# Moving small steps of a hybrid encoder block: latent scaling, first weights, rope table and buffer turns

## The chip, the cores and the metric

The kernel runs on one core of a Trainium2 chip. The core has five engines with queues of their own: TensorE (PE in the profile) multiplies matrices, VectorE (DVE) and ScalarE (ACT) work element by element, GpSimd (POOL) does small side work, and SyncE (SP) issues nearly all DMA transfers. Each engine executes its instructions in order; between engines there are only semaphores. The metric is the device time of one execution in microseconds (us), and the median of several executions is compared.

## The reference, cut to what matters

One layer of a hybrid encoder on 2048 tokens of width 1024, in float32:

```python
xn = rms_norm(h, ln_mix_g[l])
proj = xn @ w_in[l]                              # 1024 -> 2512 columns
y_a = mlstm_group(q, k, v, o, gates + b_gates)   # 4 heads x 128, two directions, chunks of 128
y_b = mla_group(c_q, c_kv, k_rope, ...)          # latent attention: 4 heads, latents of 256 and 128, rope 64
h = h + jnp.concatenate([y_a, y_b], axis=-1) @ w_out[l]
h = h + conv_gated_mlp(rms_norm(h, ln_ffn_g[l]), w_up[l], ..., w_down[l])    # 1024 -> 2 x 2816 -> 1024
gate = jax.nn.sigmoid(rms_norm(h, ple_norm_g[l]) @ w_ple_gate[l])
h = h + gate * rms_norm(p[l] @ w_ple_proj[l], ple_post_g[l])
return rms_norm(h, final_g)
```

Inside the latent group the two latents are normalised before anything is multiplied with them (`rms_norm(c_q, q_norm_g)` over 256 columns, `rms_norm(c_kv, kv_norm_g)` over 128), and the rope part of queries and key is turned by a table of cosines and sines, 64 numbers for each token.

## The kernel before, in words

**Precision.** Every matrix product is done in three passes: an operand is split into a rounded high part, by a cast on ACT, and a low part, by a subtraction on DVE (both in `split`, so all these casts carry line L121 and all these subtractions L124), and high x high, high x low and low x high are summed. Every weight and every operand thus costs one ACT instruction and one DVE instruction ahead of its matmuls.

**Places.** Nearly all SBUF is cut into places with fixed names (x0 to x15, w0 to w13, u0 to u2, t0 to t7, s0 to s2 ...). `self.at("x10", ...)` asks for a place, and whoever writes it has to wait until its last user is done. Which place a thing lies in therefore decides when its load or cast may start. A scheduler may bring an engine's independent instructions forward; `keep_in_program_order` pins an instruction at the place where it is written.

**Stages.** Five, one after the other on PE:

1. In-projection (`in_proj`, 0 to 205 us): 16 groups of 128 tokens. Per group `rest` takes the product with 464 columns (16 gates, latents of 256 and 128, rope 64; `wsr` in the profile, 24 matmuls), `vals` the product with 512 value columns (`wsp`, 24 matmuls), and `turn_rest` transposes the normalised latents (four transposes into `rtp`). From a rest bank, DVE takes the gates (gt, L252), ACT copies the rest scaled by the token's norm (rs, L255) and squares the two latents (L261, L262), POOL makes the reciprocal roots in three steps (L263, then `rsq`, L142 and L144, result rsr), and DVE scales the latents (nn, L265 and L266) and applies rope (L269 to L275). Beside the groups a generator, `work`, is moved on step by step: `token_sums` forms sums of token blocks for the next stage (x loaded as xsr, stored to xo_d), and `pair_begin` loads the weights of the pairs 0 and 1 (fwr) and prepares pair 0.
2. Pairs (205 to 441): queries, keys and output gate of the mLSTM are multiplied in 12 pairs by a Strassen-like scheme of seven products each (`prod`, L525). `side(at)` runs small jobs beside product number `at`: operand loads, the steps of the generator `gates`, and in the last pair `queries_begin`.
3. Queries (441 to 505): eight chunks of latents are multiplied up to queries; `rope` turns them with a table chunk qcs, `turn` transposes, and results go to DRAM (q_d) to be read back as q_t by the attention.
4. Attention (505 to 1215): 64 tiles (4 heads x 16 blocks of queries). Beside them the mLSTM runs as a generator: `pump` moves it on by `rate`, SIDE over the number of dots in a fixed order string (13) times 64, at each dot. `pause(n)` waits n such steps. Per chunk of 128 tokens it makes state (cf, cb, L990), scores, and the normalised output: squares, `rsq` on POOL, a multiply on DVE (hy, L1105), and a transpose on PE (mb, L1109).
5. Stream (1215 to 2865): 8 + 44 + 24 + 8 = 84 items of weights (output projection, up, down, gate), each seven products by the same scheme (L1678). An item's weights are split three times; `up_pair` takes the next of the five places in PAIRS each time, for the pairs of stage 2 as well:

```python
PAIRS = (("w5", "w6"), ("w8", "w9"), ("w3", "w4"), ("x10",), ("x11",))
tags = self.PAIRS[self.npair % 5]
```

The DMA queue of SP is in order as well: a store that waits for its data holds back the loads behind it.

Of the kernel before, what the change touches and what calls it, by code (L numbers as in the profile page):

```python
# [19 lines left out]
P = 128  # L20
S = 2048
D = 1024
# [15 lines left out]
SIDE = 658  # L38
# [22 lines left out]
class Block:  # L61
# [125 lines left out]
    def in_proj(self):  # L187
# [31 lines left out]
        xq, xs, nq = {}, {}, {}  # L219
# [29 lines left out]
        def rest(st, ps):  # L249
            rx = rcol[:, st:st + 1]  # L250
            for i, o in ((0, st), (8, NT - 1 - st)):
                nc.vector.scalar_tensor_tensor(self.gt[:, i:i + 8, o], ps[:, i:i + 8], rx, bg[:, i:i + 8],  # L252
                                               op0=ALU.mult, op1=ALU.add)
            rs = self.at(f"t{st % 2}", [P, 448], name="rs")
            nc.scalar.activation(rs, ps[:, 16:NREST], AF.Copy, scale=rx)  # L255
# [9 lines left out]
            nc.vector.scalar_tensor_tensor(nn[:, 0:256], rs[:, 0:256], r[:, 0:1], gn[:, 0:256], op0=ALU.mult, op1=ALU.mult)  # L265
            nc.vector.scalar_tensor_tensor(nn[:, 256:384], rs[:, 256:384], r[:, 1:2], gn[:, 256:384], op0=ALU.mult, op1=ALU.mult)  # L266
            nc.sync.dma_start(self.vv_d[:, st], nn[:, 256:384])
# [8 lines left out]

        def turn_rest(st):
            nn = nq.pop(st)
            pt = self.ppv.tile([P, 4, P], F32, name="rtp", tag="pv")
            for j in range(4):  # L280
                nc.tensor.transpose(pt[:, j, :], nn[:, j * P:(j + 1) * P], self.ident)
# [41 lines left out]
        vals(0)  # L323
        split_x(2)
        turn_rest(0)
# [6 lines left out]
        vals(1)  # L332
        work = chain(self.token_sums(), self.pair_begin())
        for st in range(2, NT):
# [7 lines left out]
            if st in (4, 6):  # L342
                norm_row(st // 2 - 2)
# [5 lines left out]
            if st < 5:  # L349
                for q in range(4 * st - 4, 4 * st):  # L350
                    square(q)
            else:
                next(work, None)
            turn_rest(st - 1)
# [4 lines left out]
            if st > 4:  # L359
                next(work, None)  # L360
            vals(st)
            if st > 4:
                next(work, None)
# [20 lines left out]
    def token_sums(self):  # L384
# [24 lines left out]
        for i in range(8):  # L409
# [7 lines left out]
            if blk:  # L417
# [5 lines left out]
                c = self.at("u2", [P, 2, SB], name="xsc")  # L423
# [25 lines left out]
    def pair_load(self, i):  # L449

        raw = []
        for e in range(2):
            t = self.at(("w12", "w13", "w0", "w1")[i % 2 * 2 + e], [P, KT, P], name="fwr")
# [24 lines left out]
    def pair_begin(self):  # L478

        self.npair = 1  # L480
        self.pair_load(0)
        self.pair_load(1)
        yield
        yield
        yield from self.pair_prep(0)

    def pairs(self):
# [94 lines left out]
        for i in range(12):  # L582
# [8 lines left out]
            def side(at):  # L591
                if i == 0 and at in (1, 2):
                    load("T3", range(2))
                if i == 0 and at in (3, 4):
                    load("T4", range(2))
                if i == 0 and at in (6, 7):
                    load("B22", range(2))
                if 0 < i < 5 and at % 2:
# [84 lines left out]
    def queries_begin(self, at, bank):  # L683
# [18 lines left out]
        if at == 5:  # L702
            self.wo = [self.split_wo(0)]
        if at == 6:
# [16 lines left out]
    def split_wo(self, h):  # L721
        t = self.at(("x3", "x7")[h % 2], [P, 2, D], F32R, "woa")
# [6 lines left out]
    def queries(self):  # L729
# [12 lines left out]
        cc, ro, cs = {}, {}, {}  # L742

        def split_c(c):
# [17 lines left out]
        def rope(c):  # L762
# [8 lines left out]
            for e in range(2):  # L771
                x1, x2 = ps[:, e, :, 0:32], ps[:, e, :, 32:64]
                cos = cs[c][:, e, 0, :].unsqueeze(1).broadcast_to([P, NH, 32])
                sin = cs[c][:, e, 1, :].unsqueeze(1).broadcast_to([P, NH, 32])
# [33 lines left out]
        with self.tc.manual_schedule(engines={mybir.EngineType.PE}):  # L808
# [7 lines left out]
            for c in range(8):  # L816
# [11 lines left out]
                if c + 2 < 8 and c:  # L828
# [4 lines left out]
                if c == 6:  # L833
# [1480 lines left out]
```

## Time and profile before

| | us |
|---|---|
| three executions | 2878.12, 2878.22, 2880.88 |
| median | 2878.22 |
| the profiled execution | 2876.04 |
| its span, first to last instruction | 2874.3 |
| mean granted TensorE clock | 0.997 |

| stage | stretch, us | PE busy, us |
|---|---|---|
| in-projection, after its start-up | 84 to 205 | 109.7 |
| pairs | 205 to 441 | 233.4 |
| queries | 441 to 505 | 56.5 |
| attention and mLSTM | 505 to 1215 | 698.5 |
| stream | 1215 to 2865 | 1641.1 |

The profile names an instruction by its line, its engine, its operation, and result <- operands. A number in square brackets is the idle time of the engine just before the instruction, with what ended it: "[1.11 <-POOL rsr L144]" says that the engine stood for 1.11 us until POOL had written rsr. In the view of the waits a line holds the engine, what it was about to work on, what it waited for, and then total us, number of times and the longest. Matmul durations overlap their successors' a little, since they are pipelined.

### The profile page before, as it was taken

How to read it: one execution, taken by the hardware profiler on the slowest of the kernel's cores; microseconds unless marked ns; L12 is line 12 of the kernel's file. 1: busy time of each engine (PE TensorE's matmuls, PEld its weight loads, DVE VectorE, ACT ScalarE, POOL GpSimd, SP SyncE). 2: the span in 40 equal slices, each digit the busy share in tenths (PEclk: the TensorE clock that was granted, in tenths of full speed). 3: DMA queues.
4: the chain of work that ended last, by engine and by line, in shares of the span. 5: the costliest groups of instructions: out<-in, count | busy, mean ns of one | idle time of the engine just before them, and what ended most of it. 6: DMA issues, size and time to landing. Idle time of an engine off the chain costs nothing.

```text
span 2874.3 us, 40054 instructions
## 1 busy us (share of the span) xinstructions
PE 2818.0 (98%) x13932; PEld 2357.9 (82%) x13932; DVE 2133.7 (74%) x3702; ACT 1581.6 (55%) x3071; POOL 211.0 (7%) x347
## 2 busy tenths in 40 slices
PE   9989998999999999999999999999999999999998
PEld 7777888888888888788888888888888788888787
DVE  4867766777777777777778877877778767676777
ACT  6336865556655666655655555655556333254665
POOL 2100000000001000034200000000000000011012
PEclk9999999999999999999999999999999999999999
DMA  8884648554333333378845544657776767586864
GB/s 270 269 260 119 198 147 248 170 180 128 126 117 108 116 109 110 130 239 276 270 139 181 196 166 156 214 180 237 237 235 201 235 194 245 167 265 206 284 201 164
DMA packets 444628, 552.73 MB, mean 192 GB/s; under 512 B 34661, under 2 KB 296841, under 8 KB 444425
## 3 DMA queue, kind: packets, MB, share of 16 engines
q1 hardware_dynamic: 444424, 550.16, 59.8%
q8 instruction: 110, 1.80, 0.3%
q14 instruction: 94, 0.76, 0.1%
HBM read 357.45 MB, written 192.61 MB: 191 GB/s over the span
## 4 chain that ended last, share of the span: by engine, by line
PE 79%; DMA 4%; DVE 3%; ACT 3%; issue 2%; POOL 0%; SPq 0%; POOLq 0%; ACTq 0%; DVEq 0%
PE fy L1678 21%; PE fz L1678 14%; PE fx L1678 14%; PE ppv L1217 3%; PE tb L1205 3%; PE bk L1142 2%; PE bk L1146 2%; PE bk L1144 2%; PE bk L1145 2%; PE bk L1143 2%; PE fy L525 2%; PE ppv L1218 2%; PE fs L134 2%; PE fx L525 1%; PE mb L1081 1%
## 5 line engine op out<-in xcount | busy, mean ns | idle before, releaser
L1678 PE MATMUL fz<-op,fw 128*128 128x512 f32 x1968 | 477.9, 391 | 4.1 <-ACT fw L121 4.0
L1678 PE MATMUL fx<-op,fw 128*128 128x512 f32 x1968 | 476.8, 390 | 3.2 <-ACT fy L1791 1.7
L1678 PE MATMUL fy<-op,fw 128*128 128x512 f32 x1968 | 475.2, 390 | 0.0
L1678 PEld LDWEIGHTS fz<-op,fw 128*128 128x128 f32 x1968 | 367.3, 188 | 81.9 <-ACT fw L121 5.1
L1678 PEld LDWEIGHTS fx<-op,fw 128*128 128x128 f32 x1968 | 368.0, 188 | 80.4 <-ACT fy L1791 2.1
L1678 PEld LDWEIGHTS fy<-op,fw 128*128 128x128 f32 x1968 | 368.6, 188 | 76.6
L121 ACT CAST pt<-tb 128x512 fp32r<-128x512 f32 x256 | 146.9, 586 | 197.8 <-PE tb L1205 196.8
L1678 PE MATMUL fy<-op,fwd 128*128 128x512 f32 (+1 forms) x984 | 238.6, 390 | 0.4 <-DVE uv L1663 0.4
L1147 DVE TENSOR_REDUCE mx<-bk 128x1 f32<-128x512 f32 x256 | 175.3, 685 | 67.3 <-PE bk L1146 64.7
L1678 PEld LDWEIGHTS fy<-op,fwd 128*128 128x128 f32 x984 | 182.5, 188 | 38.7 <-DVE uv L1663 0.8
L124 DVE TENSOR_TENSOR pt<-tb,pt 128x512 fp32r<-128x512 f32 x256 | 173.3, 685 | 34.1 <-ACT pt L121 32.7
L1217 PE MATMUL ppv<-pt,kv 128*128 128x512 f32 x512 | 188.0, 406 | 1.0 <-DVE pt L124 1.0
L1164 ACT ACTIVATE pe<-bk,nm 128x512 f32<-128x512 f32 x256 | 174.6, 697 | 15.5 <-DVE nm L1158 15.2
L124 DVE TENSOR_TENSOR fw<-fwr,fw 128x1024 fp32r<-128x1024 f32 x124 | 150.7, 1220 | 35.9 <-ACT fw L121 35.8
L121 ACT CAST op<-opr 128x512 fp32r<-128x512 f32 x205 | 120.3, 619 | 79.9 <-DMA opr<-tw_d 15.9
L121 ACT CAST fw<-fwr 128x1024 fp32r<-128x1024 f32 x124 | 129.4, 1050 | 48.6 <-DVE fwr L1652 23.0
L124 DVE TENSOR_TENSOR op<-opr,op 128x512 fp32r<-128x512 f32 x205 | 135.0, 691 | 25.8 <-ACT op L121 24.0
L1205 PE MATMUL tb<-ident,pe 128*128 128x128 f32 x1024 | 150.5, 273 | 2.2 <-DVE pt L124 1.9
L1218 PE MATMUL ppv<-pt,kv 128*128 128x256 f32 x512 | 144.1, 281 | 0.0
L1205 PEld LDWEIGHTS tb<-ident,pe 128*128 128x128 f32 x1024 | 122.3, 140 | 21.7 <-DVE pt L124 4.3
L121 ACT CAST fw<-hraw 128x1024 fp32r<-128x1024 f32 (+1 forms) x72 | 70.2, 981 | 116.2 <-PE fx L1678 59.1
L1726 DVE SCALAR_TENSOR_TENSOR fgv<-uv,fcw,fgv 128x1024 f32<-128x1024 f32 x88 | 112.8, 1282 | 16.2 <-ACT fgv L1724 15.4
(404 smaller groups left out, 5207.2 us busy)
## 6 DMA issues: line engine op xcount, KB each, us to landing
fwr<-in_w_up SPq DMA_DIRECT2D x66, 512.0 KB, 5.0
fh<-h_d SPq DMA_DIRECT2D x48, 512.0 KB, 4.1
h_d<-fh SPq DMA_DIRECT2D x48, 512.0 KB, 4.6
s_d<-fwr SPq DMA_DIRECT2D x44, 512.0 KB, 2.8
fws<-s_d SPq DMA_DIRECT2D x44, 512.0 KB, 3.6
rw<-row_d SPq DMA_DIRECT2D x32, 512.0 KB, 5.6
tw_d<-tsum SPq DMA_DIRECT2D x60, 256.0 KB, 5.1
opr<-tw_d SPq DMA_DIRECT2D x60, 256.0 KB, 5.1
```

The lines of the kernel that those rows point to most:

```text
L121: nc.scalar.copy(hi, src)
L124: (sub or nc.vector).tensor_tensor(lo, src, _f(hi), op=ALU.subtract)
L134: mm = lambda *a, **k: self.nc.tensor.matmul(*a, **k, skip_group_check=more)
L525: nc.tensor.matmul(out, a[:, k * P:(k + 1) * P], parts[lo], start=first, stop=lo == 1 and k == 3, skip_group_check=more)
L1142: mm(ps, ql, kh[:, ks], start=True, stop=False)
L1147: nc.vector.tensor_reduce(s.mx[:, kb:kb + 1], ps, axis=AX.X, op=ALU.max)
L1164: nc.scalar.activation(s.pe[:, kb % 2], s.banks[kb], AF.Exp, bias=s.nm, accum_out=s.rs[:, kb:kb + 1])
L1205: nc.tensor.transpose(t[:, j, :], s.p[kb][:, j * P:(j + 1) * P], self.ident)
L1217: mm(w.ps, vh[:, ks], pts[kb][:, j], start=kt == 0, stop=False, skip_group_check=True)
L1218: mm(w.ps[:, 0], vl[:, ks], pts[kb][:, j, 0], start=False, stop=kt == NT - 1, skip_group_check=True)
L1678: nc.tensor.matmul(out, a[:, k * P:(k + 1) * P], parts[lo][:, cols], start=first, stop=lo == 1 and k == last, skip_group_check=more)
L1726: nc.vector.scalar_tensor_tensor(t, u[:, tap:tap + 2 * SB], self.taps[:, tap, ct:ct + 1], t, op0=ALU.mult, op1=ALU.add)
```

## The change

Several small edits, in the order of the stages.

- **In-projection.** ACT copies the whole rest bank (464 columns, not 448) at once, and the gates are taken by DVE from that copy instead of from the bank. The factor 1/128 moves into the second square, which removes one POOL step per group. The scaling of the latents and its store leave `rest` for a new function `finish`, called behind `vals`; its first multiply is pinned, the second is not. The turns of the first group come after the second group's values; in the last two groups both scalings come behind the values of group 14. `token_sums` starts half a group to a group earlier, and its buffer xsc alternates between two places.
- **Pair 0's weights** are loaded at group 7 into x10, one place for both halves. Its preparation is split into three parts, of which the third comes in the first product of the pairs. The turn of the five places starts at another point. The loads of T3, T4 and B22 move some products later, and `gates` starts and yields later.
- **Queries.** The rope table for all eight chunks is loaded by two transfers into x7 in the last pair, in place of one small load per chunk; `split_wo` uses x6; the first output-weight product takes another bank; chunk 7 is split earlier; an Exp on one number is issued on ACT at chunk 3.
- **Attention side.** The first chunk pauses 8 steps, not 5; the normalising multiply is pinned and comes two steps after its square chain, not one; SIDE is 678, not 658.
- **Stream.** The turn of places starts over at w5, w6 when the attention begins.

```diff
@@ in_proj
         def rest(st, ps):
-            rx = rcol[:, st:st + 1]
+            whole = self.at(f"t{st % 2}", [P, NREST], name="rs")
+            nc.scalar.activation(whole, ps[:, :NREST], AF.Copy, scale=rcol[:, st:st + 1])
             for i, o in ((0, st), (8, NT - 1 - st)):
-                nc.vector.scalar_tensor_tensor(self.gt[:, i:i + 8, o], ps[:, i:i + 8], rx, bg[:, i:i + 8],
-                                               op0=ALU.mult, op1=ALU.add)
-            rs = self.at(f"t{st % 2}", [P, 448], name="rs")
-            nc.scalar.activation(rs, ps[:, 16:NREST], AF.Copy, scale=rx)
+                nc.vector.tensor_tensor(self.gt[:, i:i + 8, o], whole[:, i:i + 8], bg[:, i:i + 8], op=ALU.add)
+            rs = whole[:, 16:NREST]
...
-            nc.scalar.activation(nn[:, 256:384], rs[:, 256:384], AF.Square, accum_out=ssq[:, 1:2])
-            nc.gpsimd.tensor_scalar(ssq[:, 1:2], ssq[:, 1:2], 1.0 / 128, None, op0=ALU.mult)
-            r = self.rsq(ssq, 2, 1.0)
-            nc.vector.scalar_tensor_tensor(nn[:, 0:256], rs[:, 0:256], r[:, 0:1], gn[:, 0:256], op0=ALU.mult, op1=ALU.mult)
-            nc.vector.scalar_tensor_tensor(nn[:, 256:384], rs[:, 256:384], r[:, 1:2], gn[:, 256:384], op0=ALU.mult, op1=ALU.mult)
-            nc.sync.dma_start(self.vv_d[:, st], nn[:, 256:384])
+            nc.scalar.activation(nn[:, 256:384], rs[:, 256:384], AF.Square, scale=128.0 ** -0.5, accum_out=ssq[:, 1:2])
+            fin[st] = nn, rs, self.rsq(ssq, 2, 1.0)
...
+        def finish(st):
+            nn, rs, r = fin.pop(st)
+            a = nc.vector.scalar_tensor_tensor(nn[:, 0:256], rs[:, 0:256], r[:, 0:1], gn[:, 0:256], op0=ALU.mult, op1=ALU.mult)
+            self.tc.keep_in_program_order(a)
+            nc.vector.scalar_tensor_tensor(nn[:, 256:384], rs[:, 256:384], r[:, 1:2], gn[:, 256:384], op0=ALU.mult, op1=ALU.mult)
+            nc.sync.dma_start(self.vv_d[:, st], nn[:, 256:384])
...
+            if st == 7:
+                self.pair_load(0)
...
-            turn_rest(st - 1)
+            if st < NT - 1:
+                turn_rest(st - 1)
             if st == NT - 2:
                 continue
             if st == NT - 1:
                 vals(st - 1)
+                finish(st - 1)
+                finish(st)
+                turn_rest(st - 1)
-            if st > 4:
+            if st > 3:
                 next(work, None)
             vals(st)
+            if st < NT - 1:
+                finish(st)
@@ pair_load, pair_begin, pairs
+        both = self.at("x10", [P, 2, KT, P], name="fwr") if i == 0 else None
...
-        self.npair = 1
-        self.pair_load(0)
+        self.PAIRS, self.npair = (("w3", "w4"), ("x11",), ("w5", "w6"), ("w8", "w9"), ("x10",)), -1
         self.pair_load(1)
+        self.begun = self.pair_prep(0)
+        next(self.begun)
...
-                if i == 0 and at in (1, 2):
+                if i == 0 and at == 1:
+                    next(self.begun)
+                if i == 0 and at in (2, 3):
                     load("T3", range(2))
...
-                if 0 < i < 5 and at % 2:
+                if (1, 4) < (i, at) < (5, 0) and at % 2:
@@ queries
+            self.qcs = self.at("x7", [P, 8, 2, 64], name="qcs")
+            for e in range(2):
+                nc.sync.dma_start(self.qcs[:, :, e], self.d["rope"].rearrange("(c t p) a b -> t p c (a b)", t=2, p=P)[e])
...
-            t = cs[c] = self.at("s2", [P, 2, 2, 32], name="qcs")
-            nc.sync.dma_start(t, d["rope"][c * 256:(c + 1) * 256].rearrange("(t p) a b -> p t a b", p=P))
...
-                ps = self.bank()
+                ps = self.bank() if h else self.gbank()
...
+                if c == 3:
+                    self.tc.keep_in_program_order(nc.scalar.activation(self.stat(1, "warm"), self.nhalf[:, 0:1], AF.Exp))
@@ mlstm, attend
             if c == 0:
-                yield from pause(5)
+                yield from pause(8)
...
-            yield
-            nc.vector.tensor_tensor(hh, hh, r4.unsqueeze(2).broadcast_to([P, NH, P]), op=ALU.mult)
+            yield from pause(2)
+            a = nc.vector.tensor_tensor(hh, hh, r4.unsqueeze(2).broadcast_to([P, NH, P]), op=ALU.mult)
+            self.tc.keep_in_program_order(a)
...
+        self.PAIRS, self.npair = Block.PAIRS, -1
```

What this does to the order of instructions shows at three places. The first is DVE in the in-projection, from one eviction of values (vo) on; op and xsr are the token sums' work, xh the low part of the next tokens, gt the gates, sc the rope's products. Before:

```order
L289 TENSOR_SCALAR vo<-bk,rcol 128x512
L124 TENSOR_TENSOR xh<-x_t,xh 128x1024
L439 TENSOR_TENSOR xsr<-xsr 128x512
L415 SCALAR_TENSOR_TENSOR xsr<-xsr,gcol,rrow 128x1024
L124 TENSOR_TENSOR op<-xsr,op 128x512
L441 TENSOR_TENSOR xsr<-xsr 128x512
L252 SCALAR_TENSOR_TENSOR gt<-bk,rcol,bg 128x8 x2
L445 TENSOR_TENSOR xsr<-xsr 128x512
L415 SCALAR_TENSOR_TENSOR xsr<-xsr,gcol,rrow 128x1024
L269 TENSOR_TENSOR sc_1163<-rs,sc_1163 128x32
L265 SCALAR_TENSOR_TENSOR nn<-rs,rsr,gn 128x256
L266 SCALAR_TENSOR_TENSOR nn<-rs,rsr,gn 128x128
```

and after, where the scaling nn is L274 (256 columns) and L276 (128 columns):

```order
L293 TENSOR_SCALAR vo<-bk,rcol 128x512
L269 TENSOR_TENSOR nn<-sc_961 128x32
L274 SCALAR_TENSOR_TENSOR nn<-rs,rsr,gn 128x256
L270 COPY nn<-nn 128x64
L124 TENSOR_TENSOR xh<-x_t,xh 128x1024
L429 SCALAR_TENSOR_TENSOR xsr<-xsr,gcol,rrow 128x1024
L124 TENSOR_TENSOR op<-xsr,op 128x512
L450 TENSOR_TENSOR xsr<-xsr 128x512
L124 TENSOR_TENSOR op<-xsr,op 128x512
L253 TENSOR_TENSOR gt<-rs,bg 128x8 x2
L276 SCALAR_TENSOR_TENSOR nn<-rs,rsr,gn 128x128
L124 TENSOR_TENSOR op<-xsr,op 128x512
```

The 256-column scaling has moved from behind the gates to behind the eviction vo, where it belongs to the group before; the 128-column scaling, which is not pinned, still stands close behind the gates, ahead of the eviction.

The second is PE at the end of the in-projection, the rest products of the groups 14 and 15, the turns (rtp) and the last values (wsp). Before:

```order
L134 MATMUL bk<-wsr,xh 128x464 x24
L281 MATMUL rtp<-ident,nn 128x128 x4
L134 MATMUL bk<-wsr,xh 128x464 x24
L281 MATMUL rtp<-ident,nn 128x128 x4
L134 MATMUL bk<-wsp,xh 128x512 x48
L281 MATMUL rtp<-ident,nn 128x128 x4
```

and after:

```order
L134 MATMUL bk<-wsr,xh 128x464 x24
L283 MATMUL rtp<-ident,nn 128x128 x4
L134 MATMUL bk<-wsr,xh 128x464 x24
L134 MATMUL bk<-wsp,xh 128x512 x30
L283 MATMUL rtp<-ident,nn 128x128 x4
L134 MATMUL bk<-wsp,xh 128x512 x18
L283 MATMUL rtp<-ident,nn 128x128 x4
```

The turn of group 14 stood between rest and values; it now stands 30 matmuls into the last 48.

The third is DVE in the attention around the normalising multiply of one chunk (hy<-hy,rsr); mx and pt are the attention's maxima and low parts, cf the state. Before:

```order
L1170 TENSOR_REDUCE gt<-rs 128x1
L1171 RECIPROCAL gt<-gt 128x1
L1147 TENSOR_REDUCE mx<-bk 128x1
L1226 TENSOR_TENSOR ya<-ya,ppv 128x256
L1147 TENSOR_REDUCE mx<-bk 128x1
L1105 TENSOR_TENSOR hy<-hy,rsr 128x512
L124 TENSOR_TENSOR pt<-tb,pt 128x4x128
L990 SCALAR_TENSOR_TENSOR cf<-cf,cols,mb 128x129 x2
L1147 TENSOR_REDUCE mx<-bk 128x1
```

and after:

```order
L1010 SCALAR_TENSOR_TENSOR cf<-cf,cols,mb 128x129 x2
L124 TENSOR_TENSOR pt<-tb,pt 128x4x128
L1010 SCALAR_TENSOR_TENSOR cf<-cf,cols,mb 128x129 x2
L1168 TENSOR_REDUCE mx<-bk 128x1
L124 TENSOR_TENSOR pt<-tb,pt 128x4x128
L1168 TENSOR_REDUCE mx<-bk 128x1
L1125 TENSOR_TENSOR hy<-hy,rsr 128x512
L1179 TENSOR_REDUCE nm<-mx 128x1
L124 TENSOR_TENSOR pt<-tb,pt 128x4x128 x2
```

The state updates cf, which stood behind the multiply, now stand in front of it, so the multiply comes later in the chunk.

More of the change, by code (lines that the diff above doesn't have):

```diff
@@ L37 @@
 LAG_T, LAG_X, LAG_R = 1, 2, 2
-SIDE = 658
+SIDE = 678
 KSCALE = 128.0 ** -0.5
@@ L280, in turn_rest @@
             for j in range(4):
-                nc.tensor.transpose(pt[:, j, :], nn[:, j * P:(j + 1) * P], self.ident)
+                t = nc.tensor.transpose(pt[:, j, :], nn[:, j * P:(j + 1) * P], self.ident)
+                if j == 0:
+                    self.tc.keep_in_program_order(t)
             rt = self.at("t6", [P, 4, P], name="rt")
@@ L451, in pair_load @@
         raw = []
+        both = self.at("x10", [P, 2, KT, P], name="fwr") if i == 0 else None
         for e in range(2):
-            t = self.at(("w12", "w13", "w0", "w1")[i % 2 * 2 + e], [P, KT, P], name="fwr")
+            t = self.at(("w12", "w13", "w0", "w1")[i % 2 * 2 + e], [P, KT, P], name="fwr") if i else both[:, e]
             self.nc.sync.dma_start(t, self.w_tile(i % 6, e))
@@ L591, in side @@
             def side(at):
[L592 removed]
+                if i == 0 and at == 1:
+                    next(self.begun)
+                if i == 0 and at in (2, 3):
                     load("T3", range(2))
[L594 removed]
+                if i == 0 and at in (5, 6):
                     load("T4", range(2))
[L596 removed]
+                if i == 1 and at in (1, 2):
                     load("B22", range(2))
[L598 removed]
+                if (1, 4) < (i, at) < (5, 0) and at % 2:
                     self.gate_bank = prev.spare if at % 2 else s.spare
```

30 lines of the change are left out of this document (15 added, 15 removed).

## The prediction

> **What bounds the kernel now.** I read the page's engine table first, then the span by stages, then the whole list of TensorE's waits.
>
> ```profile
> PE 2818.0 (98%) x13932; PEld 2357.9 (82%) x13932; DVE 2133.7 (74%) x3702; ACT 1581.6 (55%) x3071; POOL 211.0 (7%) x347
> ```
>
> TensorE (PE) is busy for 98% of the span. The change leaves its instructions as they are (13,484 in the program before and after), so only the 2% in which it is not busy, and time that a slow clock adds to its matmuls, can go or grow. The stages follow; the columns are us, busy time and count of PE, its weight loads, DVE, ACT and POOL, then granted clock, DMA share, GB/s.
>
> ```profile
> 108.00:120.00 12.00, 11.16 (x52) 9.38 (x52) 10.89 (x24) 5.36 (x11) 1.17 (x3) 1.00 0.78 253
> 156.00:168.00 12.00, 11.11 (x52) 9.09 (x51) 8.29 (x20) 2.84 (x7) 1.14 (x3) 1.00 0.92 292
> 180.00:192.00 12.00, 6.67 (x29) 5.39 (x30) 5.66 (x21) 4.24 (x9) 1.33 (x3) 0.87 0.92 247
> 192.00:205.00 13.00, 13.00 (x53) 10.54 (x52) 9.85 (x21) 6.51 (x13) 1.39 (x3) 0.86 0.78 216
> 441.00:505.00 64.00, 56.47 (x388) 51.62 (x387) 42.09 (x134) 31.95 (x60) 0.00 (x0) 0.95 0.81 242
> 505.00:1215.00 710.00, 698.49 (x4298) 605.59 (x4298) 544.09 (x1323) 426.86 (x1176) 45.20 (x64) 1.00 0.41 128
> ```
>
> Two stretches of the in-projection and the queries' stage show a clock below 1.00. The waits, for the whole span (us in total, times, longest):
>
> ```profile
> PE rtp L281 <- DVE nn L265: 6.7, 4, 5.2
> PE bk L1142 <- DVE q_s L124: 4.7, 1, 4.7
> PE rtp L281 <- DVE nn L275: 4.2, 7, 1.3
> PE fz L1678 <- ACT fw L121: 4.0, 2, 2.4
> PE mb L1109 <- DVE hy L1105: 4.0, 4, 1.7
> PE bk L134 <- DVE xh L124: 2.9, 2, 1.5
> PE mb L986 <- DVE cb L990: 2.6, 1, 2.6
> PE fx L1678 <- ACT fy L1791: 1.7, 1, 1.7
> PE fx L1678 <- ACT fw L121: 1.4, 1, 1.4
> PE fs L914 <- DVE mg L910: 1.4, 1, 1.4
> PE mb L986 <- DVE cf L990: 1.4, 1, 1.4
> PE fy L525 <- ACT ug L625: 1.0, 1, 1.0
> PE bk L134 <- ACT uv L562: 0.5, 1, 0.5
> ```
>
> **A. In-projection: the latents' scaling behind the values' eviction, and pair 0's weights at x10.** PE works a group of 128 tokens in about 11.2 us (below, from one values group's start to the next, 12.45, less the 1.27 it waited). VectorE (DVE) holds it back:
>
> ```profile
> 96.23 5.73 PE L134 MATMUL bk<-wsp,xh 128*128 128x512 f32 x24
> ...
> 108.60 0.33 PE L281 MATMUL rtp<-ident,nn 128*128 128x128 f32 x1 [1.27 <-DVE nn L275]
> 108.68 5.71 PE L134 MATMUL bk<-wsp,xh 128*128 128x512 f32 x24
> 109.73 0.75 DVE L289 TENSOR_SCALAR vo<-bk,rcol 128x512 f32<-128x512 f32 x1
> 114.53 0.36 DVE L252 SCALAR_TENSOR_TENSOR gt<-bk,rcol,bg 128x8 f32<-128x8 f32 x2
> 117.90 0.49 DVE L265 SCALAR_TENSOR_TENSOR nn<-rs,rsr,gn 128x256 f32<-128x256 f32 x1 [1.11 <-POOL rsr L144]
> 121.66 0.74 DVE L289 TENSOR_SCALAR vo<-bk,rcol 128x512 f32<-128x512 f32 x1
> ```
>
> From one values eviction to the next DVE takes 11.93 us, of which 1.11 are spent standing at the scaling for POOL. That wait exists because the square chain starts only after DVE has come round to the gates, 3.37 us before the scaling. After the change ACT copies the group's bank as soon as PE ends it, so the chain runs while DVE does other work, and DVE needs 10.82 against PE's 11.2. The margin of 0.4 is thin, but the scheme balances itself: DVE meets the chain too early only when it is ahead. The scaling now stands behind the eviction of the group's values, and PE's turn of that group comes one rest product after those values, about 5 us (11.2 less the values' 5.73 and the turn's four transposes). Eviction 0.74 and scaling 0.49 leave DVE about 3.8 us of lag before the turn waits. POOL's removed step only shortens a chain that is no longer waited for: 0.
>
> The stage's end is a different loss:
>
> ```profile
> 183.65 1.05 ACT L121 CAST fw<-fwr 128x1024 fp32r<-128x1024 f32 x1 [6.88 <-DMA fwr<-in_w_in]
> 184.73 1.23 DVE L124 TENSOR_TENSOR fw<-fwr,fw 128x1024 fp32r<-128x1024 f32 x1 [3.95 <-ACT fw L121]
> 191.50 13.15 PE L134 MATMUL bk<-wsp,xh 128*128 128x512 f32 x48
> ```
>
> ACT and DVE stood in order behind pair 0's weights, and PE's turn behind them. Now these weights are loaded with group 7, and the last two groups' scalings stand behind the values of group 14. I remove the 5.2. The 48 matmuls after it took 13.15 where two groups of 24 take 11.46: 1.69 of slow clock goes too. In all A can free 6.7 + 4.2 + 1.4 of the 2.9 (the longest, 1.5, lies at the kernel's start, before any of this) + 1.7 = 14.0. What may be late next is data: compressing the stage asks more of the DMA.
>
> ```profile
> DMA packets 29066, 29.39 MB, mean 272 GB/s; under 512 B 2937, under 2 KB 21121, under 8 KB 29059
> ```
>
> These 29.39 MB moved between 84 and 192. At the 292 GB/s of the fullest row above they need 100.7 us of the 108, which allows 7.3 from the waits and 1.69 from the clock: 9.0. The two 512 KB loads that come early add no bytes, but take 1.05 MB / 292 = 3.6 us of backlog where the share is 0.78 to 0.92; DVE's 3.8 us of lag just cover it. Ends 9.0 and 14.0; some of these bytes can still slip behind the stage, so I take a value between, **11**.
>
> **B. Pairs.** The third part of pair 0's preparation moves into the first product, and the loads T3, T4, B22 move to later products; the generator of gates yields once more before the product that waited 1.4 for DVE's mg. That and the 1.0 behind ACT's ug are the stage's only waits. The moved part is two casts and two subtractions of the sizes shown (1.05, 1.23) and two smaller sums; PE needs it two products later, 24 matmuls, nearly 6 us by the group of 24 above, and its data lie there by then. Ends 0 and 2.4; **2**.
>
> **C. Queries.** weights(0) takes another bank: the 0.5 goes. Eight rope loads on SP become two in the stage before; two steps of VectorE change an operand only. The 4.7 stays:
>
> ```profile
> 472.88 3.07 SPq L805 DMA_DIRECT2D q_d<-qso  x4
> 476.69 1.58 SPq L1124 DMA_DIRECT2D q_t<-q_d  x2
> 480.52 0.40 ACT L121 CAST q_s<-q_t 128x256 fp32r<-128x256 f32 x1 [2.01 <-DMA q_t<-q_d]
> 482.04 0.63 PE L1143 MATMUL bk<-kv,q_t 128*128 128x512 f32 x1
> 482.46 0.63 PE L1144 MATMUL bk<-kv,q_s 128*128 128x512 f32 x1
> ```
>
> No rope load stands in this chain of stores and the load that reads them back, and SP issues them in the same order. The early Exp pulls a table load from one idle time of ACT into another: 0. **0.5**.
>
> **D. Attention.** One instruction of DVE, and one line of DVE's waits in this stage:
>
> ```profile
> 629.00 1.29 DVE L1063 TENSOR_TENSOR qi<-qk,rw 128x512 f32<-128x512 f32 x2 [2.76 <-DMA qk<-qk_d]
> DVE hy L1105 <- POOL rsr L144: 14.3, 13, 1.9
> ```
>
> Three more steps of the side generator put qi later; PE's mb stood 2.6 behind DVE's cb, which stood behind qi. With SIDE 658 over 710 us a step is 1.08, so 3.2 us against the 2.76: gone. The normalising multiply L1105 waited for POOL in 13 of 16 chunks, holding the exponentials' subtractions behind it; one more step (1.08) and its pinned place cover most waits (mean 1.1, longest 1.9). That frees up to 4.0 + 1.4. Ends: 9 if some short waits behind DVE go too (2.6 + 5.4 + 1), 3 if the longest L1105 waits remain and the rephased side work meets new ones of their kind (four of 1.7 cancel the 5.4, and 2.6 stays gained). Nearer the upper, since 14.3 us of DVE standing go: **6**.
>
> **E. Stream.** The first weights go to w5 and w6 instead of x10, which the last attention tile held, so their casts come ahead of its last product in ACT's order. What stays is this:
>
> ```profile
> 1219.79 0.62 ACT L121 CAST op<-opr 128x512 fp32r<-128x512 f32 x1 [1.02 <-DMA opr<-to_d]
> 1220.73 0.57 ACT L1791 COPY fy<-fx 128x512 f32<-128x512 f32 x1
> ```
>
> The 1.4 goes; the 1.7 behind the copy at 1220.73 stays, since that waits for a DMA and may take back part. Ends 3.1 and -2.4 (the five places' turn is shifted for the whole stream, and its longest wait, 2.4, could come once more); **1**.
>
> **Sum.** 11 + 2 + 0.5 + 6 + 1 = 20.5 off. The profiled execution took 2876.04, 2.2 below the median of 2878.22; on the median 2857.7, said as **2858**.
>
> **Rivals.** *The data come too late:* the in-projection stays at the DMA's 272 GB/s, so the 11 shrinks to the slow clock's 1.7 and little else (I say 3): 12.5 off, **2866**. For it: share 0.92 and, at 156, DVE down to 8.29 of 12; against it: 253 GB/s in the very row where DVE is 10.89 busy, so DVE then set the pace.
>
> *The queries' chain shortens and A comes whole:* 14.0 instead of 11, and 4.7 with its clock loss. The score matmuls after that wait start 0.42 apart (482.04, 482.46); the stage's clock of 0.95 over 64 us is up to 3.2, and I take 2. The extra 3.0 + 4.7 + 2 gives 30 off, **2848**. Against: the chain above. The Trainium skill, "TensorE: Matmul & The Clock Gate", Part 1, says that one idle window of some 3.4 us halves the clock until about 3.4 us of work have passed. The trace agrees so far as it goes: the waits of 5.2 and 4.7 lie where the clock is 0.87, 0.86 and 0.95, and the stage of the 2.6 has 1.00. By that rule, cutting the 4.7 by 1.3 would be enough to free the 2 as well: 3.3 in all, an estimate by that page, which no run here shows yet.
>
> *Slower, by the stream's places:* each of the stream's 84 items of weights is split three times, into five places in turn, and the change shifts the turn. If that puts, at one item in seven, the place that comes free late under a cast that PE needs at once, 12 casts wait like the longest now, 2.4: 29 lost against 20.5 won, 8.5 slower, **2887**. It passes 0.2% slower from 11 such waits, and with 7 to 10 the kernel is within 0.2%. Against: in the present turn three of 252 splits made PE wait (4.0 in two, 1.4 in one).
>
> **How the numbers follow.** 0.2% (5.8 us) is about what a measurement can tell from no change. Forecast 0.52; data too late 0.20; queries too 0.14; places slower 0.07, places cancelling the gain 0.07. Faster 0.86, same 0.07, slower 0.07. The forecast's own range, by the ends of A, D and E, is 2850 to 2866; the data rival at its worst (A at 0, D at 3) leaves 2872, the queries' one reaches 2848. I give 2847 to 2873.
>
> **What would show it.** Right: the turns' waits in the in-projection under 3 in total and no clock below 1.00 before 205; no 6.9 at ACT; DVE's L1105 (now L1125) hardly waiting for POOL; the 2.6 gone; the 4.7 still there within 0.7. Wrong: DVE waiting for xsr or x_t between 84 and 192 with PE's turns behind it; waits of over 1 us at mb in other tiles; PE waiting for fw casts at more than three pairs of the stream.

## The result, and the profile after

The changed kernel takes 2857.67 us (median of four, 2855.55 to 2859.16) against 2878.17 for the kernel before: a ratio of 0.9926, 95% interval 0.9909 to 0.9943. The forecast was 2858. That the total agrees says little yet, since five terms stand behind it; so the profiled executions (2876.04 and 2859.16) are first cut at the same instructions of TensorE (PE): the first matmul of the pairs, of the queries, of the scores, and of the stream.

| stretch, us | before | after | difference | forecast |
|---|---|---|---|---|
| up to the first pair's matmul (A) | 204.85 | 193.08 | -11.8 | -11 |
| pairs (B) | 236.62 | 236.17 | -0.4 | -2 |
| queries, up to the first score (C) | 39.97 | 40.95 | +1.0 | -0.5 |
| first score to the stream (D) | 734.86 | 730.80 | -4.1 | -6 |
| stream (E) | 1648.45 | 1646.88 | -1.6 | -1 |
| sum | | | -16.9 | -20.5 |

The two profiled executions differ by 16.9, the medians by 20.5: the one after is the longest of its four, the one before is below all four that make the median of before. A term of 1 or 2 us is therefore not settled by these two alone.

The waits of TensorE in the whole span after the change (us in total, times, longest):

```profile
PE bk L1163 <- DVE q_s L124: 6.8, 1, 6.8
PE tb L298 <- POOL rcol L144: 4.5, 2, 2.6
PE fz L1700 <- ACT fw L121: 3.8, 3, 2.3
PE mb L1130 <- DVE hy L1125: 2.2, 3, 1.0
PE mb L1130 <- DVE v L988: 1.9, 1, 1.9
PE fy L541 <- ACT ug L643: 1.6, 1, 1.6
PE qpr L134 <- DVE nm L1179: 1.6, 1, 1.6
...
PE tb L1227 <- DVE pt L124: 1.3, 5, 0.6
...
PE fs L944 <- DVE ms L939: 0.7, 1, 0.7
```

The turns of the latents (rtp), 10.9 us before, are gone from the list, and so are cb, cf and the stream's two waits at fx. New are 4.5 at tb<-rcol, a transpose of the tokens' norms, and 1.9 at mb behind v. The wait for q_s, 4.7 before, is 6.8. By stretches (PE, its weight loads, DVE, ACT, POOL with counts, granted clock, DMA share, GB/s):

```profile
72.00:84.00 12.00, 12.00 (x52) 10.30 (x51) 9.46 (x14) 5.66 (x13) 1.05 (x2) 0.88 0.67 234
...
108.00:120.00 12.00, 12.00 (x58) 10.33 (x58) 10.84 (x25) 5.05 (x11) 0.89 (x2) 1.00 0.91 283
...
132.00:144.00 12.00, 12.00 (x60) 10.32 (x59) 8.59 (x20) 3.90 (x10) 1.67 (x2) 1.00 0.98 337
...
470.00:493.00 23.00, 21.22 (x124) 18.82 (x125) 13.48 (x41) 6.70 (x16) 0.00 (x0) 0.91 0.60 174
```

From 84 to 193 PE never stands still: a group takes 10.95 us. DVE is as busy as before in the busy rows (10.84 of 12), and the DMA carries 337 GB/s at a share of 0.98 without a wait of PE. In this execution the slow clock has moved from the in-projection's end to 72 to 84, behind the second norm transpose (the forecast had none before 205), and stays behind the wait for q_s. Of the five other kernels below whose in-projection is the same code, four have 1.00 in that row.

### The profile page after: what moved, and what is told of

It is laid out like the page before. It is cut to its first block, busy times and chain, and to the rows that moved or that the text cites. A ratio compares the mean times of both kernels' runs of the same rounds, so it can differ in the third digit from the quotient of the medians.

```text
span 2857.4 us, 39996 instructions
## 1 busy us (share of the span) xinstructions
PE 2816.5 (99%) x13932; PEld 2363.5 (83%) x13932; DVE 2131.6 (75%) x3702; ACT 1581.6 (55%) x3072; POOL 211.1 (7%) x331
## 4 chain that ended last, share of the span: by engine, by line
PE 84%; DVE 4%; DMA 3%; ACT 2%; issue 1%; POOL 0%; SPq 0%; POOLq 0%; ACTq 0%; DVEq 0%
PE fy L1700 22%; PE fz L1700 15%; PE fx L1700 14%; PE ppv L1239 4%; PE tb L1227 3%; PE fy L541 3%; PE fz L541 2%; PE ppv L1240 2%; PE bk L1163 2%; PE bk L1165 2%; PE bk L1166 2%; PE bk L1164 2%; PE bk L1167 2%; PE fx L541 2%; PE fs L134 2%; PE mb L1101 1%
## 5 line engine op out<-in xcount | busy, mean ns | idle before, releaser
L1185 ACT ACTIVATE pe<-bk,nm 128x512 f32<-128x512 f32 x256 | 174.7, 698 | 21.2 <-DVE nm L1179 21.1
```

Source lines behind the costliest of these rows:

```text
L1185: nc.scalar.activation(s.pe[:, kb % 2], s.banks[kb], AF.Exp, bias=s.nm, accum_out=s.rs[:, kb:kb + 1])
```

## The experiments

Each kernel was measured beside the kernel before on the same chip. The last column is by how much its median lies below that of before, which was 2878.17, 2875.14, 2875.88 and 2875.07 in the four series; the intervals are worth about 4 to 5 us, so differences of 1 to 3 us between two rows are no findings by themselves.

| kernel | median, us | ratio to before (95%) | below before, us |
|---|---|---|---|
| the change | 2857.67 | 0.9926 (0.9909 to 0.9943) | 20.5 |
| scaling back in rest | 2858.86 | 0.9942 (0.9928 to 0.9957) | 16.3 |
| gates first | 2856.49 | 0.9932 (0.9917 to 0.9946) | 18.7 |
| pair 0's weights late | 2855.98 | 0.9929 (0.9912 to 0.9946) | 19.2 |
| norms later | 2854.05 | 0.9924 (0.9909 to 0.9938) | 21.1 |
| two places for qso | 2852.26 | 0.9920 (0.9905 to 0.9935) | 23.6 |
| q_t early | 2845.58 | 0.9897 (0.9882 to 0.9911) | 30.3 |
| queries back | 2856.23 | 0.9933 (0.9918 to 0.9948) | 19.7 |
| stream's turn back | 2856.60 | 0.9939 (0.9922 to 0.9956) | 19.3 |
| both halves of the latents' edit back | 2866.01 | 0.9965 (0.9952 to 0.9978) | 9.1 |
| the in-projection's end back | 2855.96 | 0.9932 (0.9918 to 0.9947) | 19.1 |
| attention's edits back | 2856.51 | 0.9931 (0.9916 to 0.9946) | 18.6 |
| q_t early, two qso, norms moved | 2848.39 | 0.9905 (0.9888 to 0.9921) | 26.7 |

### The latents: each half alone, then both

The scaling back in rest, behind the chain, not pinned:

```diff
             fin[st] = nn, rs, self.rsq(ssq, 2, 1.0)
+            finish(st)
...
         vals(0)
-        finish(0)
```

> The changed kernel with the scaling of the latents and its store back inside rest, right behind the square chain and not pinned; ACT still copies the whole bank first, the gates still come from that copy. Theory (the chain's start is what mattered: ACT no longer waits for DVE's gates): the chain is ready early enough wherever the scaling stands, PE's turns hardly wait, 2857 to 2861. Rival (the place behind the eviction is what mattered): DVE stands 1 us or more per group in front of the eviction again, the turns wait as before the change, 2864 to 2868.

Measured: 2858.86, inside the theory's range, but 16.3 below before where the change has 20.5. The trace of its longest execution (2862.29) does not bear the theory out: DVE stands at the scaling seven times, 6.0 us in all, and late in the stage a turn waits, with a slow product behind it (24 matmuls in 7.75 us, not 5.72):

```profile
171.64 0.48 PE L283 MATMUL rtp<-ident,nn 128*128 128x128 f32 x1 [3.67 <-DVE nn L271]
171.77 7.75 PE L134 MATMUL bk<-wsp,xh 128*128 128x512 f32 x24
```

The in-projection ends at 201.69 there, against 188.4 to 193.1 in the six kernels, the change among them, whose in-projection is the change's.

The gates from the bank first, the scaling left behind the eviction:

```diff
-            whole = self.at(f"t{st % 2}", [P, NREST], name="rs")
-            nc.scalar.activation(whole, ps[:, :NREST], AF.Copy, scale=rcol[:, st:st + 1])
+            rx = rcol[:, st:st + 1]
             for i, o in ((0, st), (8, NT - 1 - st)):
-                nc.vector.tensor_tensor(self.gt[:, i:i + 8, o], whole[:, i:i + 8], bg[:, i:i + 8], op=ALU.add)
-            rs = whole[:, 16:NREST]
+                nc.vector.scalar_tensor_tensor(self.gt[:, i:i + 8, o], ps[:, i:i + 8], rx, bg[:, i:i + 8],
+                                               op0=ALU.mult, op1=ALU.add)
+            rs = self.at(f"t{st % 2}", [P, 448], name="rs")
+            nc.scalar.activation(rs, ps[:, 16:NREST], AF.Copy, scale=rx)
```

> The changed kernel with the gates taken by DVE from the bank ahead of ACT's copy, as before the change; the scaling stays behind the eviction. Theory (the chain's start mattered): the chain starts only when DVE comes to the gates, DVE stands about 1 us per group at the scaling it brings forward, and the turns wait: 2861 to 2867. Rival (the place behind the eviction alone is enough, since eviction and splits cover 3.4 us of chain): 2856 to 2860.

Measured: 2856.49, the rival's range, with the in-projection's end at 191.73. By the medians each half alone costs 4.2 and 1.8 us, no more than the intervals. So both were undone together (the two diffs above in one kernel):

> The changed kernel with both halves of the latents' edit undone: gates from the bank ahead of ACT's copy, and the scaling back inside rest; pair 0's early weights and the rest stay. Each half alone cost little when it was undone (1.8 and 4.2 us less gain). Theory (either half alone keeps DVE from standing in front of a late chain; without both it stands 1 us per group again and the turns wait): 5 to 8 us of the gain of some 20 are lost, so 12 to 15 less than the kernel before. Rival (neither half matters, the groups' waits went with the sums' earlier start and second buffer): 17 to 20 less.

Measured: 9.1 below before, so 11.4 of the gain went: more than the theory had said, and not where the theory put it. In that kernel DVE stands at the scaling again (its waits between 75 and 205):

```profile
DVE nn L276 <- POOL rsr L144: 11.1, 11, 1.5
```

and yet the eight turns between 78 and 156 do not wait at all. PE waits at one turn, late in the stage, and is slow behind it (24 matmuls in 8.08 us, not 5.72):

```profile
158.93 0.69 DVE L439 TENSOR_TENSOR xsd<-xsr,xsc 128x512 f32<-128x512 f32 x1 [2.48 <-DMA xo_d<-xsd]
162.16 1.28 DVE L424 SCALAR_TENSOR_TENSOR xsr<-xsr,gcol,rrow 128x1024 f32<-128x1024 f32 x1 [2.53 <-DMA xsr<-in_x_turned]
...
166.91 0.59 PE L284 MATMUL rtp<-ident,nn 128*128 128x128 f32 x3 [0.40 <-DVE nn L276]
171.14 0.48 PE L284 MATMUL rtp<-ident,nn 128*128 128x128 f32 x1 [3.64 <-DVE nn L272]
171.26 8.08 PE L134 MATMUL bk<-wsp,xh 128*128 128x512 f32 x24
```

DVE lost 5 us to the sums' transfers within one group, and had no room for them. This is the stall of the kernel with the scaling alone back, and the stage ends where it ended there, at 201.41: in these two traces the place of the scaling matters and the order of the gates adds nothing. Why the medians are 7 us apart all the same is not shown. The changed kernel meets late transfers too, one group apart, without a wait of PE:

```profile
139.90 0.69 DVE L444 TENSOR_TENSOR xsd<-xsr,xsc 128x512 f32<-128x512 f32 x1 [2.45 <-DMA xo_d<-xsd]
155.15 1.29 DVE L429 SCALAR_TENSOR_TENSOR xsr<-xsr,gcol,rrow 128x1024 f32<-128x1024 f32 x1 [2.69 <-DMA xsr<-in_x_turned]
160.18 0.74 DVE L293 TENSOR_SCALAR vo<-bk,rcol 128x512 f32<-128x512 f32 x1
```

What differs is how far DVE lags behind PE, read at the eviction vo against the end of its values product: before the change 5.3 us at 71, 7 to 8 from the first sums to 146, then 5 to 6.4. With the scaling back, alone or with the gates, it grows from 1.3 or 1.6 at 86 to over 5, and to 6.8 or 6.9 behind the late transfers. After the change it is 0 to 3, and 1.6 to 3.2 with the gates first. So the place of the scaling decides whether DVE falls behind from group to group, and that is cashed when a transfer is late.

### The end of the in-projection

Pair 0's weights late, everything else as changed:

```diff
-            if st == 7:
-                self.pair_load(0)
...
+        self.pair_load(0)
         self.pair_load(1)
```

> The changed kernel with the weights of pair 0 loaded at the end of the token sums instead of at group 7 (same place x10). Theory (ACT and DVE stand behind these weights, PE's last turns behind them): 5.2 + 1.4 of waits and 1.7 of slow clock come back, some 8 us, 2864 to 2867, with ACT waiting 5 us or more for fwr. Rival (the new order of the last two groups, with values between rest and turns, hides the weights): 2857 to 2860.

Measured: 19.2 below before, the rival's side: in its time 2855.98, under both ranges. The late weights hold ACT for 2.05 us, not for 6.88 as before:

```profile
171.65 1.05 ACT L121 CAST fw<-fwr 128x1024 fp32r<-128x1024 f32 x1 [2.05 <-DMA fwr<-in_w_in]
```

With the turn of group 14 moved ahead of the values too:

```diff
-            if st < NT - 1:
-                turn_rest(st - 1)
+            if st == NT - 1:
+                finish(st - 1)
+            turn_rest(st - 1)
             if st == NT - 2:
                 continue
             if st == NT - 1:
                 vals(st - 1)
-                finish(st - 1)
                 finish(st)
-                turn_rest(st - 1)
```

> The changed kernel with both edits at the in-projection's end undone: pair 0's weights loaded late, and the turn of group 14 asked for ahead of the values of group 14 (the scheduler lets ten of their matmuls pass). Theory (late weights hold ACT and DVE, but PE only notices when a turn stands early; the new order hid them in the run with late weights alone): 5 to 8 us are lost, 12 to 15 less than the kernel before, with a wait of 3 us or more at the turn and a slow stretch behind it. Rival (the scaling alone took the turn out of the weights' way): 17 to 20 less.

Measured: 19.1 below before, the rival again. The turn of group 14 does not wait; the only turn that does is one at 121, 1.2 us. With the rest of the change in place, neither edit at the stage's end is needed to keep the 5.2 away, as far as this run goes back: the turn stands ten matmuls into the values here, and stood in front of them before the change.

### The norms' transposes

```diff
-            if st in (3, 5):
-                norm_row(st // 2 - 1)
...
             rest(st, nat(st, wr, NREST))
+            if st in (3, 5):
+                norm_row(st // 2 - 1)
```

> The changed kernel with the transposes of the token norms issued behind the rest product of groups 3 and 5, instead of in front of it. PE waited 4.5 us at these two transposes, and the rest product after the second took 6.83 against 5.20. Theory: both waits and the slow stretch go, 6 us, 2850 to 2853. Rival (the norms are simply late, and DVE's sums wait for the row of norms instead and hand the wait on to PE): 2855 to 2858.

Measured: 21.1 below before, 0.6 more than the change. PE's wait at the transposes is gone, and two turns wait instead, 0.7 and 1.9:

```profile
PE rtp L283 <- DVE nn L274: 1.9, 1, 1.9
```

The rival describes it better: the 4.5 had given DVE time to come up with the first sums. Without it DVE's lag is 5.6 us at 82, where the change has 2.1 at 85; it then falls to 0.8 by 124.

### The wait for q_s

Two places for the turned rope parts:

```diff
-            so = self.at("w0", [P, 2, 2, 256], F32R, "qso")
+            so = self.at(("w0", "w13")[c % 2], [P, 2, 2, 256], F32R, "qso")
```

> The changed kernel with the turned rope parts of the queries (qso) in two places by turns instead of one. In the changed kernel ACT stood 1.7 and 2.4 us at qso in front of the loads of q_t, and PE then 6.8 for q_s. Theory (the one place and its stores' way to DRAM set the chain): the wait of 6.8 falls by 2 to 4 us, 2853 to 2856. Rival (SP's issue of the stores, 2.6 to 3.9 us for each chunk's four, sets it): within 1 us of the changed kernel, 2856.5 to 2859.

Measured: 23.6 below before, the wait at q_s 5.0 instead of 6.8. That is 1.8 off the wait, just short of the theory's 2 to 4: the one place is part of the chain, not the whole of it.

All edits of the queries' stage undone (rope table by chunks, split_wo at x7, the bank, chunk 7's place, no early Exp):

> The changed kernel with all edits of the queries' stage undone (rope table by chunks, the bank of the first output weights, chunk 7's place, no early Exp). The wait for q_s grew from 4.7 to 6.8 with the change. Theory (PE comes 1.5 us earlier to an unchanged chain of stores and loads, so the wait only takes up what was gained in front of it): the wait is 5 to 6, the time 2856 to 2859. Rival (one of these edits made the chain longer): the wait is back at 4.7 or less and the kernel faster by 1 to 3, 2854.5 to 2856.5.

Measured: 2856.23, 19.7 below before; the wait is 5.4, with 1.3 and 0.6 at earlier places of the stage, 7.3 together against 6.8. The time lies in both ranges, and the waits speak for the theory: what is gained in front of this chain is waited at its end.

The two loads of q_t one chunk earlier:

```diff
         load_q(0, 0)
         load_q(0, 1)
+        yield
         split_q(0, 0)
...
+                if c == 3:
+                    att = self.attend_begin()
+                    next(att)
                 if c == 4:
                     self.kr2, self.krl = kr
-                    att = self.attend_begin()
                     next(att)
```

> The changed kernel with the first two loads of q_t issued one chunk of queries earlier. They need chunks 0 and 1 only, but stand on SP behind the stores of chunks 3 and 4. Theory (the place in SP's order sets the wait of 6.8): the wait falls to under 3 us, and with it the slow matmuls after it: 5 to 8 us gained, 2850 to 2853. Rival (q_t is only the last in a row; the casts of q_s then wait for ACT or the scores for other operands): 0 to 2 us gained, 2855.5 to 2858.

Measured: 2845.58, 30.3 below before, 9.8 more than the change and beyond the theory's 5 to 8. The load and what PE does then, first after the change, then with q_t early:

```profile
465.40 1.54 SPq L1145 DMA_DIRECT2D q_t<-q_d  x2
470.20 0.80 PE L1163 MATMUL bk<-kv,q_s 128*128 128x512 f32 x1 [6.82 <-DVE q_s L124]
470.79 0.63 PE L1164 MATMUL bk<-kv,q_t 128*128 128x512 f32 x1
471.22 0.63 PE L1165 MATMUL bk<-kv,q_s 128*128 128x512 f32 x1
```

```profile
454.38 1.43 SPq L1147 DMA_DIRECT2D q_t<-q_d  x2
459.69 0.50 PE L1165 MATMUL bk<-kv,q_s 128*128 128x512 f32 x1 [1.73 <-DVE q_s L124]
460.02 0.39 PE L1166 MATMUL bk<-kv,q_t 128*128 128x512 f32 x1
460.25 0.40 PE L1167 MATMUL bk<-kv,q_s 128*128 128x512 f32 x1
```

The wait is 1.7 and the score matmuls come 0.23 apart at once, not 0.43. In the profiled executions the queries' stretch is 35.95 (40.95 after the change) and the next 725.27 (730.80 after the change, which is the longest of the ten kernels with the changed attention and an unmoved q_t; the shortest has 727.58).

### Attention and stream

```diff
-SIDE = 678
+SIDE = 658
...
-                yield from pause(8)
+                yield from pause(5)
...
-            yield from pause(2)
-            a = nc.vector.tensor_tensor(hh, hh, r4.unsqueeze(2).broadcast_to([P, NH, P]), op=ALU.mult)
-            self.tc.keep_in_program_order(a)
+            yield
+            nc.vector.tensor_tensor(hh, hh, r4.unsqueeze(2).broadcast_to([P, NH, P]), op=ALU.mult)
```

> The changed kernel with the attention's edits undone (pause of 5, multiply one step after its chain and not pinned, SIDE 658). Theory (they gained some 6 us): 13 to 16 less than the kernel before; DVE waits over 12 us for POOL at the multiply again, and PE's waits at mb are 6 or more. Rival (the stage's other waits move about and the edits gain nothing net): 18 to 21 less.

Measured: 18.6 below before, in the rival's range by the median; by its own stage, first score to stream, 734.25 against 730.80 after the change, and 727.58 to 730.32 in the nine other kernels here that have the changed attention behind an unmoved q_t. The waits agree with the theory. PE's at mb with the edits undone, and DVE's for POOL with and without them:

```profile
PE mb L1129 <- DVE hy L1125: 3.8, 3, 1.8
PE mb L1006 <- DVE cb L1010: 2.1, 1, 2.1
PE mb L1006 <- DVE cf L1010: 1.4, 1, 1.4
DVE hy L1125 <- POOL rsr L144: 14.5, 13, 1.9
```

```profile
DVE hy L1125 <- POOL rsr L144: 4.8, 4, 1.9
```

The stream's turn as before the change:

```diff
-        self.PAIRS, self.npair = Block.PAIRS, -1
+        self.PAIRS, self.npair = Block.PAIRS, 2
```

> The changed kernel with the stream's places starting at x10, as before the change. Theory: the last attention tile holds x10, PE waits 1.4 at the first product again and the 1.7 at the third comes back, 2858.5 to 2861. Rival (the turn makes no difference; the gain at the stream's start was the operands' timing): within 0.7 of the changed kernel.

Measured: 2856.60, 19.3 below before where the change has 20.5, and both waits at fx are back:

```profile
PE fx L1700 <- ACT fy L1813: 2.1, 1, 2.1
PE fx L1700 <- ACT fw L121: 0.9, 1, 0.9
```

Its stream takes 1649.89 in the profile, 3.0 more than after the change, which is what the two waits sum to. But the changed stream takes 1646.2 to 1649.6 in the other kernels, so the waits are shown and the 3.0 of time is not.

### Together

q_t early, qso in two places, the first norm transpose behind group 3's rest product and the second at group 6:

> The changed kernel with q_t loaded one chunk earlier, qso in two places, the first transpose of the norms behind group 3's rest product and the second at group 6 in front of the rest product. Theory (the waits at the norms go, the one for q_s stays small): 33 to 36 less than the kernel before. Rival (the norms' waits move on to the sums, qso in two places adds nothing once q_t is early): 29 to 31 less, as with the early q_t alone.

Measured: 26.7 below before, under the rival's range too, and less than q_t early alone though the intervals overlap. No norm wait is left, but a turn waits 3.1 for DVE, and the qso places add nothing. The best version found is the changed kernel with q_t early, 2845.58, ratio 0.9897 (0.9882 to 0.9911).

## Why the prediction came out

**A, 11 forecast, 11.8 measured, and the reasons only half right.** The turns' waits and the 5.2 with its slow clock went, as the sum had them; what the sum did not have is 4.5 at the norms' transposes and a rest product of 6.83 behind the second one. The list of edits ahead of the prediction leaves out that those transposes move from groups 4 and 6 to groups 3 and 5, and that the first transpose of each turn is pinned in PE's order. So the move was put at nothing, and it had a price:

```profile
46.07 0.27 PE L298 MATMUL tb<-ident,rcol 128*8 128x128 f32 x1 [2.59 <-POOL rcol L144]
46.10 5.07 PE L134 MATMUL bk<-wsr,xh 128*128 128x464 f32 x23
...
70.38 0.27 PE L298 MATMUL tb<-ident,rcol 128*8 128x128 f32 x1 [1.96 <-POOL rcol L144]
70.40 6.83 PE L134 MATMUL bk<-wsr,xh 128*128 128x464 f32 x24
```

It was paid for by small stops that the list of waits does not hold: a group was put at 11.2 us of PE, and is 10.95.

Of the two causes that were given for DVE's lateness, pair 0's weights failed: with the weights late and the turn moved most of the way back, the end does not wait 5.2 again. The 1.1 us at the scaling holds in part. It decides whether DVE's lag grows or shrinks, as the lags above show; but with both halves of the latents' edit undone the middle groups do not wait, because the lag begins there at 1.6 us. So something else had made DVE late before the change, and the sum has no term for it. Part of it came ahead of the first sums: the eviction at 71.23 was 5.3 us late, behind a scaling that had stood 3.68 for POOL. Then DVE stood at the first sums for their data, with everything else in order behind it; after the change, far less:

```profile
79.36 1.28 DVE L415 SCALAR_TENSOR_TENSOR xsr<-xsr,gcol,rrow 128x1024 f32<-128x1024 f32 x1 [5.74 <-DMA xsr<-in_x_turned]
```

```profile
73.19 2.48 DVE L429 SCALAR_TENSOR_TENSOR xsr<-xsr,gcol,rrow 128x1024 f32<-128x1024 f32 x2 [1.59 <-DMA rrow<-r_d]
```

DVE was at 91% of its time before the change, and with the 1.1 us of each group a lag once taken did not shrink, as it can with the scaling moved (5.6 to 0.8 above). Which edit took the first lag away is open. The sums start a group earlier in the run with the norms' transposes later too, and there the lag at 82 is 5.6 all the same, so the early start does not by itself keep it small. Toward the stage's end there is a further rival, the second place of xsc, since before the change DVE stood for the stores out of the one place:

```profile
DVE xsc L424 <- DMA xo_d<-xsc: 5.3, 3, 3.0
```

No run undid the earlier start, the second place or the pins of the turns alone, so the part of each is not shown. Shown is that without the latents' edit 11.4 us of the gain go, and that a turn stalls late in the stage in both traces with the scaling back (some 6 us with the slow product) and in none of the eleven with it moved. The DMA rival is refuted as a limit of rate: the data set none at 292 GB/s, since rows of 337 at a share of 0.98 show no wait of PE. A single late transfer counts all the same once DVE lags.

**B, 2 forecast, 0.4 measured.** The 1.4 at mg became 0.7 at another step of the gates, and the 1.0 at ug is 1.6 in this execution. The pairs' stretch is 233.7 to 235.7 in the twelve other kernels, so that of the profiled execution, 236.17, is at the high end and 1 to 3 us are gained as a rule.

**C, 0.5 forecast, 1.0 lost.** "The 4.7 stays" was right in kind; it took up the 0.5 and more. The chain of stores that no edit touched sets the end of this stretch, so its gains are lost there. The rival that this chain could shorten was priced at 4.7 + 2: moving two loads by one chunk gave 9.8.

**D, 6 forecast, 4.1 measured**, about 5 against the run with the edits undone (734.25 less 729.4, the mean of the changed kernel's 730.80 and the nine others'). The 2.6 and the 1.4 went, the 4.0 is 2.2, and one new wait of the forecast's kind came, 1.9 behind v. The lower end of 3 was added up wrongly: four waits of 1.7 are 6.8, which leaves 1.2 of 2.6 + 5.4.

**E, 1 forecast, 1.6 measured**, which is less than the same stream differs from kernel to kernel. By the waits 3.1 went: the 1.4 went, and so did the 1.7 that was said to stay: with the first casts out of the way ACT issues the copy fy in time, though it still stands for the same DMA in front of it:

```profile
1204.42 1.26 ACT L121 CAST op<-opr 128x512 fp32r<-128x512 f32 x2 [0.93 <-DMA opr<-to_d]
1205.59 0.58 ACT L1813 COPY fy<-fx 128x512 f32<-128x512 f32 x1
```

The slower rival did not happen: three casts made PE wait 3.8 in all, as before three made it wait 4.0 and 1.4.

Of the signs that the prediction named for being right, two did not show: the clock is below 1.00 before 205, and the wait for q_s moved by 2.1, not by 0.7 at most. One that it named for being wrong did, the 1.9 at mb.

That the total is right to a microsecond is luck: it is owed to errors of both signs of up to 2 us in these two executions, and to the spread of executions, since A alone is 11.8 to 16.5 by the six kernels with the same in-projection.

## What to carry to other kernels

An engine that is 90% busy and executes in order sheds a delay only by the little room that each round leaves it: follow its lag from round to round, which shows both what made it late and whether it recovers. Undoing an edit may show little in the time; read the trace of that run by its stage before saying that the edit did not pay. And a gain in front of a chain of stores and loads is waited at that chain's end, so move the load that ends the chain first: here that was worth nearly half as much as all the rest.

## What the runs showed of the hardware

A slow stretch of matmuls does not follow idle time by its length alone. After 1.96 us at 70.38 a product took 6.83 us, not 5.20, and after waits of 1.92 and 1.91 at the same transpose with the queries back and with the scaling back 6.86 and 6.84; after 1.92 with the gates first it took 5.27:

```profile
70.03 0.27 PE L299 MATMUL tb<-ident,rcol 128*8 128x128 f32 x1 [1.92 <-POOL rcol L144]
70.06 5.27 PE L134 MATMUL bk<-wsr,xh 128*128 128x464 f32 x24
```

After 2.59 at 46.07, 23 matmuls took 5.07, the normal pace; after 3.64 in the run with both halves undone 8.08, not 5.72. The Trainium skill, "TensorE: Matmul & The Clock Gate", Part 1, speaks of an idle window of about 3.4 us that runs freely, and a wait of 1.96 is shorter than that; the stretch from 72 to 84 has a granted clock of 0.88 all the same, and the measurement stands.

The in-projection of one and the same code ended between 188.4 and 193.1 us in six kernels of these runs, which is wider than three of the five terms that the forecast was made of.
